# Where the last squares of a norm are added, and which PSUM banks three projection jobs of an indexer use

## The chip, the cores and the metric

The kernel runs on one core of a Trainium2 chip. The metric is the device time of one execution, in microseconds. A core has several engines, each with its own queue of instructions: TensorE (PE, matrix products; its weight loads are listed as PEld), VectorE (DVE), ScalarE (ACT), GpSimd (POOL) and SyncE (SP, which issues DMAs). Matrix products are written to PSUM, which is divided into banks; the other operands lie in SBUF. An engine that needs what another makes waits on a semaphore.

## What is computed

A decoder trunk of two layers, 512 tokens (T) of 1024 features (D), in float32. Each layer has a half-step SwiGLU (inner width 2816), a mixer, and another half-step SwiGLU; layer 0's mixer is a hybrid of an SSD and an mLSTM group, layer 1's is sparse attention with an indexer that picks 128 keys per query. Each of the six parts begins with a norm over the features.

```python
def rms_norm(x, g):
    y = x * lax.rsqrt(jnp.mean(x * x, axis=-1, keepdims=True) + EPS) * g
    return y

for l in range(2):
    x = x + 0.5 * swiglu(rms_norm(x, ffn_norm[l, 0]), ...)
    h = rms_norm(x, mix_norm[l])
    m = hybrid_mixer(h, ...) if l == 0 else sparse_attention(h, cos, sin, sa_w_in, ...)
    x = x + m
    x = x + 0.5 * swiglu(rms_norm(x, ffn_norm[l, 1]), ...)

def sparse_attention(h, ...):
    q, k, v, qi, ki, wi = split_cols(h @ w_in, (1024, 64, 64, 512, 64, 8))
    # rope and norms of q, k, qi, ki
    logits = einsum('bthd,bsd->btsh', qi, ki)
    score = einsum('btsh,bth->bts', relu(logits), wi) * idx_scale
    # causal mask; the top k keys of each query; softmax attention over these
    return o @ w_out
```

## The kernel before

**Layout.** The residual x lies transposed in SBUF: eight chunks (j = 0 to 7) of 128 features x 512 tokens. Products of float32 are made as three matmuls (`mm3`, lines 241 to 243) of a rounded part and a remainder: `form` tiles hold the two parts of a weight, `xgn` those of the normed input. A remainder is a subtraction on VectorE (L363 for weights and others, L660 for xgn), the rounded part a copy on ScalarE (L361, L657).

**Stages.** In program order: ffn00, mix0 (hybrid), ffn01, ffn10, mix1 (attention), ffn11. `Plan` collects the steps of the whole program with an estimated duration each and the keys that they read and write. `order` then walks through time: for each engine it takes, of the steps that are ready, the one that can start first, and among those the one with the earlier due time, which is propagated back from TensorE's steps. TensorE's steps keep their order within a stream (the attention stage has more than one; with them, other rules for due times hold). So a step with another cost or another dependency moves others on every engine.

**A norm that is settled late.** The mean of squares isn't awaited before the next stage's products begin: xgn is x times the gain, without the norm's factor, and the factor is multiplied in behind the products. Two functions do that for five norms (mix0, ffn01, ffn10, mix1, ffn11):

- `prep_later` (from L633) is called for two chunks at a time, as x becomes final. For each chunk it makes xgn's two parts and, on ScalarE, the square (L669). The squares of the earlier chunks are added into `ssq` by GpSimd (L356 with POOL, 128x512 or halves of it). The squares of the last call, two chunks, are kept apart in the list `ssqs`: with `ssq` that makes three operands.
- `settle_later` (L612 to L631) is called at two points of the next stage. At the first, `sums` (L327) has TensorE add over the 128 partitions: for each of four token blocks, one matmul with a column of ones for each operand, 12 for three operands. The result `pssq` is 128x4. VectorE turns it into mean + eps (L624), GpSimd raises it to the power -0.5 (L626). At the second point, TensorE transposes the factor into rows (`prow`, L336) and ScalarE copies them to `rrow` (L630), which VectorE multiplies to the products (L444 and others). In mix1 there are no rows; there ScalarE scales the columns directly (L1595).

The places of these two points are set by code: in `unit`, the first unit of an FFN stage, whose products into `pg` and `pu` go in blocks of 12 matmuls of 128x512, they come behind the blocks at positions 1 and 3, in ffn11 (`late`) behind those at 2 and 4. In the hybrid it is `unit_eight` and its column positions that set them. In mix1 they are the points around `scaled`.

**Layer 1's indexer.** In `attention`, `indexer(jobs, ks)` projects the normed input by the columns for ki, qi and wi (`iw`, widths 64 and 292). There are seven jobs, one for each token block b and half g (block 0 has one of 64 columns). The first four go together into banks of `gm`, `po` and twice `lg`, ahead of the norm's sums in mix1. Behind the sums, the last three follow one by one, each with `scaled`, its evacuation by ScalarE (L1595). Their banks are `gm`, `po`, `gm`: the third needs the bank that the first of the last three leaves. `self.bank(tag)` takes the next bank of a tag's ring; `lg` has three, `pt` two, `gm` and `po` one each. Further on `gm` is the bank of the key-value projection (`gm<-xgn,form`), `lg` that of the indexer's logits (L1665), `pt` that of the scores summed over heads (L1656), `pq` that of transposes (L1521). Then come rope on VectorE (L1507 to L1511), the diagonal weights on GpSimd (L1648), the selection of keys (L1883 and L1884 on VectorE) and the heads.

Of the kernel before, what the change touches and what calls it, by code (L numbers as in the profile page):

```python
# [13 lines left out]
ALU = mybir.AluOpType  # L14
# [4 lines left out]
NB = T // P  # L19
# [194 lines left out]
class Trunk:  # L214
# [135 lines left out]
    def t(self, us, issue, reads, writes):  # L350
        self.plan.add("tensor", us, issue, reads, writes)
# [224 lines left out]
    def unit(self, raws, stream, late, summed):  # L576

        nc, rrow = self.nc, self.rrow  # L580
        ps = self.pair("pg", "pA"), self.pair("pu", "pB")
        f = []
        for qs in ((0, 1), (2, 3)):
            for i in range(4):
                for _ in range(2 if not f else 1):
                    next(stream, None)
                xg, xgk = self.xg, self.xgk
                if len(f) < 4:
                    f.append(self.made(raws[i], i >= summed))
                j, b = f[i]  # L590
                for s in range(2):
                    col = slice(s * P, (s + 1) * P)
                    for q in qs:
                        k = 2 * q + i % 2
                        self.times(
                            *ps[i // 2], s, (j, lambda b=b, q=q, col=col: (b[:, 0, q, col], b[:, 1, q, col])),
                            lambda k=k: (xg[0][k], xg[1][k]), xgk(k), q == 0 and i % 2 == 0, q == 3 and i % 2 == 1, False, T,
                            0.693,
                        )
                if 2 * qs[0] + i in ((2, 4) if late else (1, 3)):  # L600
                    self.settle_later()
        yield
        t, tk = self.place()
        g = lambda: t()[:, 4:8].rearrange("p (s a) b -> p s (a b)", s=2)
        h = lambda: t()[:, 0:4].rearrange("p (s a) b -> p s (a b)", s=2)
        r = lambda: rrow.unsqueeze(1).to_broadcast([P, 2, T])
        gk, hk = ([tk(a + i) for i in range(4)] for a in (4, 0))
        pk = lambda ps: [(*ps[1], 0), (*ps[1], 1)]
        self.vtt(2 * T, g, ps[0][0], r, ALU.mult, gk, pk(ps[0]) + ["rrow"])
        self.s(2 * T, lambda: nc.scalar.activation(g(), g(), AF.Silu), gk, gk, AF.Silu)  # L610
        self.vtt(2 * T, h, ps[1][0], r, ALU.mult, hk, pk(ps[1]) + ["rrow"])
        self.vtt(2 * T, h, h, g, ALU.mult, hk, hk + gk)  # L612
        yield t, tk
# [20 lines left out]
    def prep_later(self, which, k, last, squares=True, half=None):  # L634

        nc = self.nc
        if k == 0 and not half:  # L640
            self.which = which
            self.xgn = [[Lazy(lambda: self.part.tile([P, 4, T], F32R, name="xgn", tag="xg")) for _ in range(2)] for _ in range(2)]
            squares4 = Lazy(lambda: self.tmp.tile([P, 4, T], F32, name="ssq", tag="ssq", bufs=1))
            self.sqs = [lambda i=i: squares4()[:, i] for i in range(4)]
            self.ssq = self.sqs[0]
            self.ssqs, self.ssqk = [(self.ssq, 0)], ["ssq"]
            self.xg = [LazyFeat(t) for t in self.xgn]
            self.xgk = lambda k: [("xg", which, i, k) for i in range(2)]
        xgn, xT, ssq = self.xgn, self.xT, self.ssq
        halves = (0, 1) if half is None else (half,)  # L650
        cols = slice(halves[0] * H, halves[-1] * H + H)
        n = cols.stop - cols.start
        for j in (k, k + 1):
            g, x = self.gain(which, j), xT[:, j, cols]
            hi, lo = (lambda i=i, j=j: xgn[i][j // 4]()[:, j % 4, cols] for i in range(2))
            hik, lok = ([("xg", which, i, j)] for i in range(2))
            self.s(n, lambda hi=hi, x=x, g=g: nc.scalar.activation(hi(), x, AF.Copy, scale=g), self.xk(j, halves), hik)  # L657

            def low(hi=hi, lo=lo, x=x, g=g, j=j):
                nc.vector.scalar_tensor_tensor(lo(), x, g, hi().bitcast(F32), op0=ALU.mult, op1=ALU.subtract)  # L660

            self.v(n, low, self.xk(j, halves) + hik, lok)
            if not squares:
                continue
            if j == 0:
                sq, sk = ssq, ["ssq"]
            else:
                sq, sk = self.sqs[1 + j % 3], [("sq", j % 3)]
            self.s(n, lambda x=x, sq=sq: nc.scalar.activation(sq()[:, cols], x, AF.Square), self.xk(j, halves), sk)  # L669
            if last:  # L670
                self.ssqs, self.ssqk = self.ssqs + [(sq, halves[0] * NB // 2)], self.ssqk + sk
            elif j:
                part = [lambda x=x: x()[:, cols] for x in (ssq, sq)]
                self.vtt(n, part[0], *part, ALU.add, ["ssq"], ["ssq"] + sk, True)
        if last:
            self.pending = 1 + squares

# [859 lines left out]
    def attention(self, nxt):  # L1537
# [9 lines left out]
        iw, last = [], len(plan.steps) - 1  # L1547
        for c0 in (QI0, QI0 + N1):
            for k0, k1 in ((0, 3), (3, 6), (6, 8)):
                if k1 == KC:  # L1550
                    plan.floor = last
                n = k1 - k0
                i, raw = self.ring("raw")
# [38 lines left out]
        def scaled(jobs):  # L1592
            for b, g, (ps, psk) in jobs:
                cols = slice(0 if b else KI - N1, N1 if b else KI - N1 + 64)
                self.s(cols.stop - cols.start, lambda b=b, g=g, ps=ps, cols=cols: act(  # L1595
                    pr[b][0]()[:, g * N1 + cols.start : g * N1 + cols.stop], ps()[:, cols], AF.Copy, scale=rcol[:, b : b + 1]
                ), [psk, "rcol"], [pr[b][1]])
# [5 lines left out]
        self.settle_later()  # L1603
        rcol = self.rcol
        scaled(jobs)
        for b, g, tag in ((2, 1, "gm"), (3, 0, "po"), (3, 1, "gm")):
            jobs = [(b, g, self.bank(tag))]
            indexer(jobs, (0, 1, 2, 3, 6, 7, 4, 5))
            scaled(jobs)
# [17 lines left out]
        for b in range(NB):  # L1627
            t, xk = pr[b]
            c0, n = (0, 9) if b else (KI, 1)
# [12 lines left out]
            n, sc, sk = (b + 1) * P, mask[b], maskk[b]  # L1642
# [320 lines left out]
```

## Time and profile before

| | us |
|---|---|
| timed, median of 3 runs | 2012.17 (2010.16 to 2013.01) |
| the profiled execution | 2003.96 |
| its span in the trace | 2002.2 |
| granted clock of TensorE, mean | 0.992 |
| VectorE / ScalarE / GpSimd busy | 1627.8 / 1264.7 / 325.0 |

In the rows of the profile a time is in microseconds from the span's start; an operation is named by the line of the kernel, the engine and `out<-in`. In a row of the timeline the first number is the start, the second how long the instructions named in it take together (xN), and what is in brackets is the idle time of the engine just before them and who released it. A matmul of the program with float32 operands gives two records, so the 12 sums of a norm are 24 records.

### The profile page before, as it was taken

To read this page: it belongs to the slowest core of one execution; us is meant where nothing else is said; L and a number is where in the kernel's file an instruction comes from. 1 tells how busy PE (TensorE), PEld (TensorE's weight loads), DVE (VectorE), ACT (ScalarE), POOL (GpSimd) and SP (SyncE) were. 2 spreads that over 40 slices of the span, in tenths; PEclk is the share of its full clock that TensorE was granted. 3 is DMA by queue.
4 is the path that set the end of the run, shared out by engine and by line. 5 is a ranking of instruction groups with operands and counts; after the bars stand their busy time and mean duration, and the time that the engine had idled before them with its cause. 6 is when DMAs were issued, how large, how long until landed. Compare 5 with 4: busy or idle time off the path is not lost.

```text
span 2002.2 us, 36425 instructions
## 1 busy us (share of the span) xinstructions
PE 1956.5 (98%) x14674; PEld 1813.3 (91%) x14674; DVE 1627.8 (81%) x2373; ACT 1264.7 (63%) x1906; POOL 325.0 (16%) x401
## 2 busy tenths in 40 slices
PE   8999999999999999999999999999999999999998
PEld 6999999799888888999998999999866588999998
DVE  6888888887888558989788998878589647988886
ACT  6666656567777545766566566666747744757564
POOL 1000002222234110000012001001414521101010
PEclk9999999999999999999999999999899999999999
DMA  8566766467769342666654466565735202666564
GB/s 221 137 157 152 176 155 161 118 166 190 198 176 262 86 117 74 162 172 162 158 149 141 111 170 161 155 174 137 188 88 116 53 17 69 158 158 169 148 170 115
DMA packets 226609, 292.89 MB, mean 146 GB/s; under 512 B 15036, under 2 KB 196488, under 8 KB 225928
## 3 DMA queue, kind: packets, MB, share of 16 engines
q1 hardware_dynamic: 200728, 199.30, 32.2%
q0 software_dynamic: 25632, 91.24, 24.2%
q8 instruction: 115, 1.88, 0.4%
q14 instruction: 54, 0.44, 0.1%
q10 hardware_dynamic: 80, 0.02, 0.0%
HBM read 192.96 MB, written 6.33 MB: 100 GB/s over the span
## 4 chain that ended last, share of the span: by engine, by line
PE 76%; DVE 8%; DMA 8%; issue 5%; ACT 1%; POOL 1%; SPq 0%; POOLq 0%; ACTq 0%; DVEq 0%
PE pA L242 9%; PE pA L241 9%; PE pA L243 9%; PE pD L241 5%; PE pD L243 5%; PE pD L242 5%; DMA form<-raw 3%; PE hm L242 2%; PE hm L243 2%; PE hm L241 2%; PE pB L241 2%; PE pB L243 2%; PE pB L242 2%; DMA raw<-in_hy_w_in 2%; DVE raw L356 2%
## 5 line engine op out<-in xcount | busy, mean ns | idle before, releaser
L363 DVE TENSOR_TENSOR form<-raw,form 128x1024 fp32r<-128x1024 f32 (+2 forms) x382 | 454.9, 1195 | 101.5 <-ACT form L361 100.0
L361 ACT ACTIVATE form<-raw 128x1024 fp32r<-128x1024 f32 (+2 forms) x382 | 392.1, 1030 | 206.0 <-DVE raw L356 142.4
L392 POOL DMA_DIRECT2D form<-raw x172 | 150.9, 879 | 1344.3 <-ACT form L391 1298.3
L356 DVE TENSOR_TENSOR raw<-raw 128x1024 f32<-128x1024 f32 (+2 forms) x281 | 333.2, 1190 | 22.8 <-DMA raw<-in_ffn_w_down 9.0
L241 PE MATMUL pA<-xf,form 128*128 128x256 f32 x1152 | 321.2, 279 | 0.0
L243 PE MATMUL pA<-xf,form 128*128 128x256 f32 x1152 | 320.7, 278 | 0.0
L242 PE MATMUL pA<-xf,form 128*128 128x256 f32 x1152 | 320.7, 278 | 0.0
L391 ACT ACTIVATE form<-raw 128x1024 fp32r<-128x1024 f32 (+1 forms) x172 | 178.2, 1037 | 161.6 <-PE pD L243 74.4
L241 PEld LDWEIGHTS pA<-xf,form 128*128 128x128 f32 x1152 | 217.2, 188 | 0.3
L243 PEld LDWEIGHTS pA<-xf,form 128*128 128x128 f32 x1152 | 217.3, 189 | 0.0
L242 PEld LDWEIGHTS pA<-xf,form 128*128 128x128 f32 x1152 | 217.0, 188 | 0.2
L242 PE MATMUL pA<-hid,form 128*128 128x256 f32 x704 | 198.2, 282 | 3.3 <-DVE hid L363 3.3
L241 PE MATMUL pA<-hid,form 128*128 128x256 f32 x704 | 198.0, 281 | 0.6 <-ACT hid L361 0.5
L243 PE MATMUL pA<-hid,form 128*128 128x256 f32 x704 | 197.2, 280 | 0.0
L393 ACT ACTIVATE form<-raw 128x1024 fp32r<-128x1024 f32 (+1 forms) x172 | 176.5, 1027 | 0.0
L241 PE MATMUL pD<-xf,form 128*128 128x256 f32 x576 | 160.3, 278 | 0.0
L243 PE MATMUL pD<-xf,form 128*128 128x256 f32 x576 | 160.2, 278 | 0.0
L242 PE MATMUL pD<-xf,form 128*128 128x256 f32 x576 | 160.2, 278 | 0.0
L356 DVE TENSOR_TENSOR ft<-ft 128x256 f32<-128x256 f32 (+2 forms) x296 | 151.3, 543 | 3.6
L242 PEld LDWEIGHTS pA<-hid,form 128*128 128x128 f32 x704 | 132.4, 188 | 5.2 <-DVE hid L363 5.1
L241 PEld LDWEIGHTS pA<-hid,form 128*128 128x128 f32 x704 | 132.6, 188 | 1.4 <-ACT hid L361 0.7
L508 ACT ACTIVATE ft<-pA 128x512 f32<-128x512 f32 x120 | 71.5, 595 | 97.7 <-PE pA L243 90.0
(441 smaller groups left out, 5427.6 us busy)
## 6 DMA issues: line engine op xcount, KB each, us to landing
form<-raw POOLq DMA_DIRECT2D x156, 512.0 KB, 5.9
raw<-in_ffn_w_gate SPq DMA_DIRECT2D x88, 512.0 KB, 3.9
raw<-in_ffn_w_up SPq DMA_DIRECT2D x88, 512.0 KB, 4.1
raw<-in_ffn_w_down SPq DMA_DIRECT2D x64, 512.0 KB, 4.0
raw<-in_hy_w_in SPq DMA_DIRECT2D x44, 512.0 KB, 4.7
raw<-in_ffn_w_down SPq DMA_DIRECT2D x32, 384.0 KB, 3.1
raw<-in_hy_w_out SPq DMA_DIRECT2D x16, 512.0 KB, 4.2
form<-raw POOLq DMA_DIRECT2D x16, 384.0 KB, 4.2
```

The lines of the kernel that those rows point to most:

```text
L241: mm(out, l[0], r[0], start=start, stop=False)
L242: mm(out, l[0], r[1], start=False, stop=False)
L243: mm(out, l[1], r[0], start=False, stop=stop)
L356: (self.p if pool else self.v)(n, lambda: e.tensor_tensor(out(), x(), y(), op=op), reads, writes)
L361: self.s(n, lambda: nc.scalar.activation(hi(), src(), AF.Copy), srck, hik)
L363: n, lambda: nc.vector.tensor_tensor(lo(), src(), hi().bitcast(F32), op=ALU.subtract), srck + hik, lok
L391: self.s(n, lambda: nc.scalar.activation(f()[:, 1], raw, AF.Copy, scale=-1.0), rawk, lok)
L392: self.plan.add("gpsimd", 0.85, lambda: nc.gpsimd.dma_start(f()[:, 1], raw, accum_op=ALU.add), rawk + lok, lok, 5.5)
L393: self.s(n, lambda: nc.scalar.activation(f()[:, 0], raw, AF.Copy), rawk, hik)
L508: self.s(T, lambda: nc.scalar.activation(to(), ps()[:, :, 0:H], AF.Copy), [(*psk, 0), (*psk, 1)], tok)
```

## The change

Three places of the code change.

```diff
@@ unit
-                if 2 * qs[0] + i in ((2, 4) if late else (1, 3)):
+                if 2 * qs[0] + i in ((2, 4) if late else (2, 3)):
                     self.settle_later()
@@ prep_later
-            if last:
-                self.ssqs, self.ssqk = self.ssqs + [(sq, halves[0] * NB // 2)], self.ssqk + sk
-            elif j:
+            if j:
                 part = [lambda x=x: x()[:, cols] for x in (ssq, sq)]
-                self.vtt(n, part[0], *part, ALU.add, ["ssq"], ["ssq"] + sk, True)
+                self.vtt(n, part[0], *part, ALU.add, ["ssq"], ["ssq"] + sk, not last)
@@ attention
-        for b, g, tag in ((2, 1, "gm"), (3, 0, "po"), (3, 1, "gm")):
+        for b, g, tag in ((2, 1, "pt"), (3, 0, "pt"), (3, 1, "lg")):
```

The squares of the last two chunks are now added into `ssq` like the others, but by VectorE; `ssqs` keeps one operand, so the sums are 4 matmuls rather than 12, and they read what VectorE added. In `unit` the first point moves one block of 12 matmuls on in ffn01 and ffn10, the second stays. The last three indexer jobs take banks of `pt`, `pt` and `lg`. All lines behind L670 move up by two: L716 of the changed kernel is L718 before, L1023 is L1021, and so on.

The plan orders the steps anew. First VectorE at mix0's norm, the end of the residuals of ffn00 (`raw<-pA`), the remainders of xgn, weight forms, and the mean (L624). Before:

```order
L718 SCALAR_TENSOR_TENSOR raw<-pA,raw 128x2x256
L660 SCALAR_TENSOR_TENSOR xgn<-raw,xgn 128x512 x4
L363 TENSOR_TENSOR form<-raw,form 128x1024
L1023 COPY raw<-hc 128x76
L363 TENSOR_TENSOR form<-raw,form 128x1024 x2
L1032 TENSOR_SCALAR raw<-raw 128x16
L624 TENSOR_SCALAR raw<-pssq 128x4
```

And of the change:

```order
L716 SCALAR_TENSOR_TENSOR raw<-pA,raw 128x2x256
L660 SCALAR_TENSOR_TENSOR xgn<-raw,xgn 128x512 x4
L363 TENSOR_TENSOR form<-raw,form 128x1024 x3
L356 TENSOR_TENSOR ssq<-ssq 128x512 x2
L363 TENSOR_TENSOR form<-raw,form 128x1024
L624 TENSOR_SCALAR raw<-pssq 128x4
L1021 COPY raw<-hc 128x76
```

The two additions stand behind three forms, and the copy of the gates (`hc`) comes behind the mean rather than two forms ahead of it. A form that stood ahead of the last four remainders before is among the three now.

Second, VectorE at ffn11's norm, where the last products of the attention's output projection (`lg`) are added to the residual. Before:

```order
L356 TENSOR_TENSOR raw<-lg,raw 128x256 x2
L660 SCALAR_TENSOR_TENSOR xgn<-raw,xgn 128x512
L356 TENSOR_TENSOR raw<-lg,raw 128x256
L660 SCALAR_TENSOR_TENSOR xgn<-raw,xgn 128x512 x3
L624 TENSOR_SCALAR raw<-pssq 128x4
```

And of the change:

```order
L356 TENSOR_TENSOR raw<-lg,raw 128x256 x2
L660 SCALAR_TENSOR_TENSOR xgn<-raw,xgn 128x512
L356 TENSOR_TENSOR raw<-lg,raw 128x256
L660 SCALAR_TENSOR_TENSOR xgn<-raw,xgn 128x512
L356 TENSOR_TENSOR ssq<-ssq 128x512 x2
L660 SCALAR_TENSOR_TENSOR xgn<-raw,xgn 128x512 x2
L624 TENSOR_SCALAR raw<-pssq 128x4
```

The additions stand behind one remainder that follows the last residual. On TensorE the sums follow directly on the last `lg` products in both; 24 matmuls into `pu` stand between sums and transposes before, and 12 of these stand ahead of the last 39 `lg` products now.

Third, TensorE at mix1's norm, from the last product of the four joint jobs (`lg`) through the sums to the next job. Before:

```order
L242 MATMUL lg<-iw,xgn 128x292
L243 MATMUL lg<-iw,xgn 128x292
L327 MATMUL pssq<-raw,ssq 128x1 x12
L241 MATMUL gm<-iw,xgn 128x292
L242 MATMUL gm<-iw,xgn 128x292
```

And of the change:

```order
L242 MATMUL lg<-iw,xgn 128x292
L243 MATMUL lg<-iw,xgn 128x292
L327 MATMUL pssq<-raw,ssq 128x1 x4
L241 MATMUL pt<-iw,xgn 128x292
L242 MATMUL pt<-iw,xgn 128x292
```

Behind this, 12 matmuls of the job stand ahead of the first transpose of ki (`pq<-raw,ri`) before, and 45 now. The first 12 matmuls of the key-value projection (`gm<-xgn,form`), which stood behind the logits of token block 1 (128x256), stand among them now; on VectorE the rope of block 3, which stood behind the first pair of the key selection, stands ahead of it; and on GpSimd the 16 diagonal weights of blocks 1 and 2 are made in one go, ahead of the DMAs of the query weights (before, 14 of them).

## The prediction

> **What bounds the kernel now.** I read the page from the top, then TensorE's waits, then the five places where a norm is settled.
>
> ```profile
> span 2002.2 us, 36425 instructions
> PE 1956.5 (98%) x14674; PEld 1813.3 (91%) x14674; DVE 1627.8 (81%) x2373; ACT 1264.7 (63%) x1906; POOL 325.0 (16%) x401
> PE 76%; DVE 8%; DMA 8%; issue 5%; ACT 1%; POOL 1%; SPq 0%; POOLq 0%; ACTq 0%; DVEq 0%
> ```
>
> TensorE (PE) is busy 1956.5 of 2002.2 us, and 76% of the chain that ends last is its own work. It can win time in three ways only: fewer instructions, fewer waits, or a higher granted clock. The next rows are those of its waits that the change comes near: what TensorE was about to run, for whom it waited, us in all, how often, and the longest.
>
> ```profile
> PE pq L1521 <- DVE q L1511: 3.7, 2, 3.0
> PE gm L242 <- DVE iw L363: 3.4, 1, 3.4
> PE pg L242 <- DVE xgn L660: 2.7, 3, 1.0
> PE hc L242 <- DVE xgn L660: 2.1, 2, 1.3
> PE pssq L327 <- POOL ssq L356: 0.9, 1, 0.9
> PE pq L1521 <- ACT ri L1533: 0.8, 1, 0.8
> ```
>
> Waits at the sums themselves (L327) come to 0.9 us. So what the sums cost is their own time on TensorE, and what they do to the clock. The first is seen at the hybrid mixer's norm (mix0):
>
> ```profile
> L327 PE MATMUL pssq<-raw,ssq x120: 164/250/352, 359.1 to 1664.4; 128*128 128x1 f32 x120
> 359.12 2.73 PE L327 MATMUL pssq<-raw,ssq 128*128 128x1 f32 x24
> 361.71 0.48 PE L241 MATMUL hm<-xgn,form 128*128 128x512 f32 x1
> ...
> 362.83 0.63 PE L242 MATMUL hm<-xgn,form 128*128 128x512 f32 x1
> ...
> 366.14 0.60 PE L336 MATMUL prow<-raw 128*128 128x128 f32 x4
> ```
>
> Each of the five norms has 24 records of one column. Here they hold TensorE 2.7 us, from 359.12 to about 361.8, or 0.112 us each. Then come 12 wide matmuls, from 361.71 to 366.14. They take 4.4 us, and from 362.83 on each lasts 0.63 us where others have 0.39 to 0.48. The windows show that this is the granted clock (columns: us, busy us of the five engines, granted clock, DMA share, GB/s):
>
> ```profile
> 1085.00:1093.00 8.00, 8.00 (x49) 7.06 (x48) 4.87 (x7) 1.14 (x2) 1.47 (x1) 1.00 0.62 197
> 362.00:366.20 4.20, 4.20 (x13) 3.19 (x12) 0.04 (x1) 0.00 (x0) 1.04 (x1) 0.59 0.30 88
> 1434.00:1445.00 11.00, 10.21 (x56) 9.35 (x55) 5.35 (x12) 6.70 (x15) 8.14 (x14) 0.69 0.68 212
> 1663.00:1672.70 9.70, 9.70 (x34) 7.99 (x35) 0.69 (x2) 0.00 (x0) 1.02 (x1) 0.65 0.01 2
> 1535.00:1570.00 35.00, 29.32 (x153) 14.66 (x151) 29.16 (x101) 31.28 (x81) 22.71 (x37) 1.00 0.27 54
> 1565.00:1580.00 15.00, 12.01 (x66) 7.52 (x63) 8.89 (x23) 9.78 (x25) 9.23 (x13) 0.89 0.00 0
> ```
>
> Behind three norms (362, 1434, 1663) the clock falls to 0.59, 0.69 and 0.65; behind ffn10's (1085) it stays at 1.00. The loss is 4.2 x 0.41 = 1.7 us, 11 x 0.31 = 3.4 us and 9.7 x 0.35 = 3.4 us. I read these as half clock, since a stretch of one-column matmuls gives the array little work. At full clock the 12 wide matmuls would take 4.4 - 1.7 = 2.7 us: the price of one block below. (The last two windows are for later.)
>
> [...] The row at 359.12 has no idle time ahead of it and the clock fell all the same, so the trace favours a window that counts work done; whether it falls then depends on the window's phase.
>
> **The change, part by part.**
>
> *Fewer sums, all five norms.* 12 matmuls of the program become 4, so 24 records become 8. 16 x 0.112 = 1.8 us is saved at each norm, 9.0 us in all, all of it on TensorE. What it costs is two additions of 128x512 on VectorE, and that the sums now wait for them. The rows of ffn01 give the sums as they stand, the nearest price of one addition, the form and the square beside it, and the power on GpSimd for all norms:
>
> ```profile
> 750.17 2.73 PE L327 MATMUL pssq<-raw,ssq 128*128 128x1 f32 x24
> 748.31 0.69 DVE L356 TENSOR_TENSOR raw<-hm,raw 128x512 f32<-128x512 f32 x1 [2.38 <-PE hm L243]
> 749.18 1.23 DVE L363 TENSOR_TENSOR form<-raw,form 128x1024 fp32r<-128x1024 f32 x1 [0.17 <-ACT form L361]
> 749.05 0.62 ACT L669 ACTIVATE ssq<-raw 128x512 f32<-128x512 f32 x1
> L626 POOL TENSOR_TENSOR raw<-raw x5: 1017/1032/1471, 362.1 to 1665.0; 128x4 f32<-128x4 f32 x5
> ```
>
> One addition is 0.7 us, a pair 1.4. VectorE, busy 81%, has ten more instructions, 7 us.
>
> *ffn01.* The last square ends at 749.7, the form at 750.4; behind it the addition ends near 751.1, and even with a microsecond lost by 752.1. By the new order one block of 12 wide matmuls, 2.7 us, is issued ahead of the sums, so TensorE reaches them near 750.17 + 2.7 = 752.9 and doesn't wait. Behind the sums only one block is left to cover the mean (0.2 us) and the power on GpSimd (L626, 1.0 to 1.5 us): 2.7 us against at most 1.7 and the handing over. I take **1.6 us**, 0.2 being lost where pg waits for a later L660 (bounds 1.1, if a whole addition of 0.7 is lost so, and 1.8).
>
> *ffn10.* The additions stand ahead of the last two L660 before the mean. TensorE's sums, the last L660s and the last squares of before are
>
> ```profile
> 1085.14 2.74 PE L327 MATMUL pssq<-raw,ssq 128*128 128x1 f32 x24
> 1085.92 2.06 DVE L660 SCALAR_TENSOR_TENSOR xgn<-raw,xgn 128x512 fp32r<-128x512 f32 x3
> 1083.76 1.16 ACT L669 ACTIVATE ssq<-raw 128x512 f32<-128x512 f32 x2 [1.74 <-DVE raw L718]
> ```
>
> The squares are there at 1084.9. One L660 and the pair end at 1085.92 + 0.7 + 1.4 = 1088.0. TensorE came to the sums at 1085.1 and comes one block later now, 1087.8. The wait is 0.2, and the mean, behind two more L660 on VectorE, is ready near 1089.5; the power takes up to 1.5 more, 1091.0, while TensorE reaches the transposes (L336) at 1088.0 + 0.9 + 2.7 = 1091.6. 1.8 - 0.2 gives **1.6 us** (0.1 if the mean is a form and a power of 1.5 us later, 1.8 if all is hidden).
>
> *mix0.* Here the sums keep their place, and VectorE has three forms (L363) ahead of the additions, one more than stands below behind the last L660s.
>
> ```profile
> 352.41 3.10 DVE L660 SCALAR_TENSOR_TENSOR xgn<-raw,xgn 128x512 fp32r<-128x512 f32 x3
> 356.72 2.34 DVE L363 TENSOR_TENSOR form<-raw,form 128x1024 fp32r<-128x1024 f32 x2
> 357.04 0.62 ACT L669 ACTIVATE ssq<-raw 128x512 f32<-128x512 f32 x1
> ```
>
> If the forms end as now, at 359.06, the additions end at 360.45, and the sums that stood at 359.12 wait 1.35 us. One form that stood ahead of the last L660s stands behind them now, and so the wait of hc for xgn (2.1 us in all) can shrink by up to its 1.2 us (2.34 for two). Without the fall of the clock the transposes come at 360.5 + 0.9 + 2.7 = 364.1, or 2.0 us earlier, and 3.2 with the earlier start; with the fall, 1.7 less: 0.3 to 1.5. I take no fall, since the work lost to sums shrinks from 2.7 to 0.9 us, and the middle: **2.5 us** (0.3 to 3.2).
>
> *mix1.* TensorE doesn't wait for the additions: VectorE idles 8 us there.
>
> ```profile
> 1432.66 0.16 DVE L624 TENSOR_SCALAR raw<-pssq 128x4 f32<-128x4 f32 x1 [8.03 <-PE pssq L327]
> 1429.89 2.73 PE L327 MATMUL pssq<-raw,ssq 128*128 128x1 f32 x24
> 1435.72 0.48 PE L1521 MATMUL pq<-raw,ri 128*128 128x128 f32 x1 [0.79 <-ACT ri L1533]
> ```
>
> 1.8 us of sums go. The three projection jobs with banks of their own run on behind the sums, 45 matmuls in a row ahead of the first pq (before, 12), so the 0.8 us wait is gone too. With a full window behind the sums the 3.4 us of half clock go: 6.0 us by the time of the indexer's logits. Late next are the heads, 1535 to 1570, where TensorE has 29.3 of 35 us busy and VectorE 29.2, ScalarE 31.3. The order also moves 12 wide matmuls (2.7 us) of the key-value product ahead, out of the stretch in which they covered VectorE. So I take 1.5 us as given back: **4.5 us** (1.1, where clock stays low and part is given back, to 6.0).
>
> *ffn11.* TensorE has 12 wide matmuls ahead of the last block of the out projection, where before it had them behind the sums, and then nothing between that block and the sums.
>
> ```profile
> 1661.16 3.55 PE L327 MATMUL pssq<-raw,ssq 128*128 128x1 f32 x24 [0.88 <-POOL ssq L356]
> 1672.62 0.60 PE L336 MATMUL prow<-raw 128*128 128x128 f32 x4
> 1660.32 0.42 DVE L356 TENSOR_TENSOR raw<-lg,raw 128x256 f32<-128x256 f32 x1 [0.35 <-PE lg L243]
> 1660.84 0.63 ACT L669 ACTIVATE ssq<-raw 128x512 f32<-128x512 f32 x1 [0.19 <-DVE raw L356]
> ```
>
> From the end of the block (1661.16 - 0.88 = 1660.28) to the transposes are 12.3 us. In the new order: 2.7 for the moved block, then a wait for residual (0.4), square (0.6) and the pair (1.4) with some 0.3 us of handing over, 2.7 in all, then 0.9 of sums and 2.7 of the other block: 9.0 us, 3.3 less. But 2.7 us of idleness and 0.9 of sums are as long a lull as 0.9 and 2.7 were, and cost half clock again: 3.4 us if as long as now (0.1 us slower), 1.7 if for half of it (1.6 faster). Between these two, **0.7 us** (-0.1 to 3.3).
>
> *The rest.* On VectorE the residuals (L718) and forms around 1410 change places, ahead of the 3.4 us wait of gm for iw; as many stand ahead of each iw form as before, within one. I take 0 (bounds 0.7 either way, one L718). GpSimd loses nothing but order; its diagonals move ahead of the weights' DMAs.
>
> The sum is 1.6 + 1.6 + 2.5 + 4.5 + 0.7 = **10.9 us**. The profiled execution took 2003.96 us, span 2002.2 and 1.8 around it, and lies 8.2 us under the median of the timed ones; I take the gain off both: 1993.1 profiled, 2012.2 - 10.9 = **2001.3 us** timed.
>
> **Rivals.**
>
> *The clock doesn't follow the sums.* For it: behind two norms of five the clock did not fall although the sums were the same, and the phase of the windows shifts with everything ahead. Then mix0 and mix1 keep their loss, 1.7 and 3.4 us, the latter partly given back already: 10.9 - 1.7 - 2.6 = 6.6 us, 2005.6. [...]
>
> *All falls vanish.* ffn11 gets 3.3, mix1 its 6.0 and mix0 3.2: with 1.6 twice 15.7 us, 1996.5. For it: the lulls shrink everywhere but in ffn11; against it: ffn11's.
>
> *It comes to nothing.* The sums are shorter but wait for VectorE at every norm: 1.35 in mix0, and as much in ffn01 and ffn10 when L660 or a form stands longer ahead of the additions; the heads give back the rest, for they are bound by VectorE and ScalarE. That is 9.0 - 3 x 1.35 - 2.7 = 2.2 us, 2010.0. Against it: ACT's squares and the idle 8 us of VectorE in mix1.
>
> *Slower.* The heads at 1535 to 1570 wait for VectorE's ropes (L1511) and what the key-value product covered is used up sooner. Idle time there is 5.7 us now, with one wait of 3.0. Each wait over about 3 us also brings 1.7 us of half clock (1565 to 1580: 15 x 0.11, with the wait of 3.0 in it). The gain of 10.9 is undone if 11 us are added there, which takes three waits of 2 us more, each with a fall; 2.7 us of moved matmuls don't pay for that. Four such waits would be 4 x 3.7 = 14.8 us, 2016.1.
>
> **How the numbers follow.** I give the forecast 0.45, the rival with the clock unmoved 0.22, all falls gone 0.14, nothing 0.13, slower 0.06. The range goes from 1993.5, the third case with the bounds of the rest, to 2009.5, near the fourth: it leaves out some 0.2. A measurement of this kernel can tell about 0.2%, 4 us, from no change: the first three cases lie beyond it, so faster 0.81, within 0.13, slower 0.06.
>
> **What would show it.** L327 x40 rather than x120, and ten additions of 0.7 us on ssq. Of the clock: 1.00 in the windows behind mix0's and mix1's sums, and a fall behind ffn11's. Of the waits: TensorE for ssq on VectorE 1 to 1.4 us in mix0 and near 2.7 in ffn11, none for L626; the pq wait on ri gone. If the sums wait in ffn01 or ffn10, or idle time at 1535 to 1570 grows by over 3 us, my terms there are wrong; if the clock falls behind mix1's sums as before, its cause is.

## The result, and the profile after

| | before | changed |
|---|---|---|
| timed, median, first measure of both (6 runs each) | 2011.16 us | 1991.32 us |
| ratio of that measure, 95% interval | | 0.9893 (0.987 to 0.9916) |
| ratio of a second and a third measure | | 0.9935 (0.9914 to 0.9956), 0.9921 (0.9895 to 0.9947) |
| all executions of the experiments: mean, median | 2007.8, 2007.6 us (87 of them) | 1992.8, 1992.6 us (23) |
| mean granted clock of these executions | 0.9913 | 0.9936 |
| profiled execution, its span | 2003.96, 2002.2 us | 1992.64, 1990.8 us |

The kernel became faster, by 15.0 us between the means (0.75%, standard error 1.0), where 10.9 was forecast. The time lies just below the range (1993.5 to 2009.5). The two profiled executions differ by 11.3 us; single executions scatter by more than that, from 1996.8 to 2020.2 us before and from 1986.4 to 2003.1 changed.

The page of the changed kernel, the lines that answer to those of before:

```profile
span 1990.8 us, 36264 instructions
PE 1944.0 (98%) x14594; PEld 1800.1 (90%) x14594; DVE 1631.5 (82%) x2383; ACT 1268.3 (64%) x1906; POOL 320.2 (16%) x401
PE 78%; DVE 8%; DMA 7%; issue 4%; ACT 1%; POOL 1%; ACTq 0%; DVEq 0%; POOLq 0%; SPq 0%
```

TensorE has 80 records fewer, VectorE ten instructions more, and TensorE's own work still sets the end. TensorE's waits that answer to those shown of before are these (what it was about to run, for whom it waited, us, times, longest):

```profile
PE pssq L327 <- DVE ssq L356: 4.0, 2, 2.9
PE pA L243 <- DVE form L363: 3.4, 1, 3.4
PE pg L242 <- DVE xgn L660: 2.5, 3, 1.0
PE hc L242 <- DVE xgn L660: 1.8, 2, 1.0
PE gm L242 <- DVE oh L1832: 1.5, 1, 1.5
```

The wait for `iw` near 1414 has only changed its name (pA for a form, 3.4 us again). New is the wait of the sums for VectorE's additions, 4.0 us in two places (before, they waited 0.9 us for GpSimd). Gone are the waits of pq for q (3.7 us) and for ri (0.8). The sums and additions themselves, by line and tile:

```profile
L327 PE MATMUL pssq<-raw,ssq x40: 164/250/250, 360.5 to 1657.1; 128*128 128x1 f32 x40
L356 DVE TENSOR_TENSOR ssq<-ssq x10: 678/688/694, 359.0 to 1655.5; 128x512 f32<-128x512 f32 x10
```

40 records in place of 120, ten additions of 0.69 us. And the windows behind the norms, with the granted clock in the third column from the end:

```profile
360.40:364.40 4.00, 3.89 (x22) 3.35 (x23) 1.48 (x4) 0.00 (x0) 1.05 (x1) 1.00 0.22 64
1430.00:1445.00 15.00, 15.00 (x110) 13.98 (x109) 5.39 (x13) 9.26 (x20) 10.57 (x18) 1.00 0.73 198
1535.00:1570.00 35.00, 31.94 (x179) 17.33 (x180) 31.33 (x102) 32.71 (x85) 23.50 (x33) 1.00 0.16 31
1565.00:1580.00 15.00, 15.00 (x93) 9.31 (x94) 9.67 (x28) 12.17 (x23) 8.58 (x12) 1.00 0.55 131
1656.00:1661.00 5.00, 4.66 (x18) 3.87 (x19) 1.59 (x4) 0.00 (x0) 1.03 (x1) 0.66 0.00 0
```

Behind mix0's and mix1's sums the clock stays at 1.00 now (before: 0.59 and 0.69 in such windows). Behind ffn11's it still falls. In the heads, 1535 to 1570, TensorE is busy 31.9 us of 35 rather than 29.3, and the fall behind 1570 is gone.

### The profile page after: what moved, and what is told of

Read it like the earlier page. It is cut to its first block, busy times and chain, and to the rows that moved or that the text cites. A ratio compares the mean times of both kernels' runs of the same rounds, so it can differ in the third digit from the quotient of the medians.

```text
span 1990.8 us, 36264 instructions
## 1 busy us (share of the span) xinstructions
PE 1944.0 (98%) x14594; PEld 1800.1 (90%) x14594; DVE 1631.5 (82%) x2383; ACT 1268.3 (64%) x1906; POOL 320.2 (16%) x401
## 4 chain that ended last, share of the span: by engine, by line
PE 78%; DVE 8%; DMA 7%; issue 4%; ACT 1%; POOL 1%; ACTq 0%; DVEq 0%; POOLq 0%; SPq 0%
PE pA L242 9%; PE pA L243 9%; PE pA L241 9%; PE pD L243 5%; PE pD L241 5%; PE pD L242 5%; DMA form<-raw 3%; PE hm L241 3%; PE hm L242 3%; PE hm L243 3%; PE pB L241 2%; PE pB L243 2%; PE pB L242 2%; DVE form L363 2%; PE pg L242 1%
## 5 line engine op out<-in xcount | busy, mean ns | idle before, releaser
L242 PEld LDWEIGHTS pA<-hid,form 128*128 128x128 f32 x704 | 132.7, 188 | 6.1 <-DVE hid L363 6.0
L243 PEld LDWEIGHTS pA<-hid,form 128*128 128x128 f32 x704 | 132.9, 189 | 3.6 <-DVE form L363 3.6
L241 PEld LDWEIGHTS pA<-hid,form 128*128 128x128 f32 x704 | 133.0, 189 | 2.2 <-ACT hid L361 1.1
```

Of the source, the lines that this page charges most:

```text
L241: mm(out, l[0], r[0], start=start, stop=False)
L242: mm(out, l[0], r[1], start=False, stop=False)
L243: mm(out, l[1], r[0], start=False, stop=stop)
```

## The experiments

Twelve runs; the table gives them all but the clock kernel, which is no version of the trunk. "Full clock" is the time multiplied by the granted clock of the same execution, and so roughly what is left without the clock's losses; for before it is 1990.2, for the changed kernel 1980.0 us. The ratio is to executions of before that ran beside the kernel, in the same job.

| run | executions | mean us | clock | full clock us | ratio, 95% interval |
|---|---|---|---|---|---|
| before again (e0) | 12 | 2008.6 | 0.9908 | 1990.2 | 1.0009 (0.9988 to 1.0031) |
| banks only (e1) | 12 | 1999.9 | 0.9925 | 1984.9 | 0.9966 (0.995 to 0.9982) |
| squares only (e2) | 7 | 1995.7 | 0.9934 | 1982.5 | 0.9941 (0.992 to 0.9962) |
| squares and settling points (e3) | 8 | 1996.1 | 0.9936 | 1983.4 | 0.9948 (0.9929 to 0.9966) |
| changed, again (f1) | 9 | 1995.1 | 0.9930 | 1981.2 | 0.9935 (0.9914 to 0.9956) |
| changed, a third time (g0) | 8 | 1991.6 | 0.9941 | 1979.9 | 0.9921 (0.9895 to 0.9947) |
| changed, sums three times (f4) | 12 | 2006.4 | 0.9912 | 1988.7 | 0.9988 (0.9967 to 1.0008) |
| before, other order, 1.40 (f5) | 12 | 2000.8 | 0.9928 | 1986.4 | 0.9963 (0.9944 to 0.9983) |
| before, other order, 1.30 (g2) | 12 | 1999.6 | 0.9921 | 1983.8 | 0.9962 (0.9943 to 0.9981) |
| changed, other order, 1.40 (g4) | 10 | 1995.4 | 0.9937 | 1982.8 | 0.9937 (0.9913 to 0.9961) |
| changed, block put back (g1) | 6 | 1988.5 | 0.9947 | 1977.8 | 0.9905 (0.9872 to 0.9937) |

### Before, again

No edit.

> The kernel before, run again as a kernel of its own, so that its executions come with their granted clock. The two profiled executions differ by 11.3 us, the timed medians by about 20. Theory A (the profiled execution of before happened to lose less clock than its timed ones): mean clock of these executions near 0.988, against 0.991 to 0.997 for the changed kernel's, and time falling by about 1.5 to 2 us for each 0.001 of clock; a second profile shows its half-clock stretches at other places than the first. Theory B (the spread comes from waits for DMA): clock about as high as the changed kernel's, 0.992 to 0.996, and no tie between clock and time.

Its twelve executions go from 1997.01 us at a clock of 0.994 to 2019.55 at 0.988; a line through them falls 2.5 us for each 0.001 of clock, one through the 26 of before in that job 1.8. So the clock carries most of the scatter: theory A holds in that, and the forecast's profile, at 0.992, was one of the better executions. The mean clock, 0.9908, lies between what the two theories asked for. And the second profile has its half clock at the places of the first, behind the sums of mix0, mix1 and ffn11 (in the first at 362.6, 1434.4 and 1663.1 us), in the hybrid (615.2), ahead of mix1's sums (1417.3) and in the heads (1570.9), with ffn10's sums as the one new place; other places had been expected. But the first three timings (median 2012.17) were above the 2007.6 of all, and the pooled clock differs from the changed kernel's by 0.0023 only, some 4.7 us. The clock alone doesn't make 15.

### One part of the change alone

Banks only (e1):

```diff
-        for b, g, tag in ((2, 1, "gm"), (3, 0, "po"), (3, 1, "gm")):
+        for b, g, tag in ((2, 1, "pt"), (3, 0, "pt"), (3, 1, "lg")):
```

> Before with only the three PSUM banks changed: sums, squares and the settling points as before. By the prediction's terms the banks save the 0.8 us wait of pq and at most part of mix1's half clock: 1 to 3 us faster than before (ratio 0.9985 to 0.9995). Rival (the attention's new order is where the gain comes from): 8 us or more faster (ratio 0.996 or lower), with the gain in the heads after 1530 us.

0.9966, or 7 to 8 us: between the two numbers and far nearer to the rival's. On TensorE its order is that of before up to mix1's sums, so the gain lies behind them: from these sums to the end its profile takes 565.2 us, that of before 572.3.

Squares only (e2):

```diff
-            if last:
-                self.ssqs, self.ssqk = self.ssqs + [(sq, halves[0] * NB // 2)], self.ssqk + sk
-            elif j:
+            if j:
...
-                self.vtt(n, part[0], *part, ALU.add, ["ssq"], ["ssq"] + sk, True)
+                self.vtt(n, part[0], *part, ALU.add, ["ssq"], ["ssq"] + sk, not last)
```

> The last squares added by VectorE, 4 sums in place of 12 per norm; the settling points and the banks as before. By the prediction's terms: 9.0 us of sums, less waits for the additions of 1.4 us in mix0, about 2 in ffn01 and 2.9 in ffn10 (which now have no block ahead of the sums), and some clock: 5 to 9 us faster (ratio 0.9955 to 0.9975), with L327 waiting for VectorE's ssq in ffn01 and ffn10. Rival (clock is the gain): 12 us or more faster, mean clock 0.994 or more.

0.9941, 12 us: more than the forecast's terms give, at the rival's lower end, and the clock (0.9934) is just under what the rival asked. The sums wait for VectorE 5.3 us in three places, 2.6 of it in ffn11, 1.1 in mix0 and 1.7 in ffn10; I had put about 6 on ffn01, ffn10 and mix0 alone, so those waits were overrated.

Squares and settling points (e3): as e2, with `(2, 3)` for `(1, 3)` in `unit`.

> Squares and settling points changed, banks as before. By the prediction's terms about 10.9 less the banks' 1 to 3 us: 8 to 10 us faster than before (ratio 0.995 to 0.996), the waits of L327 in ffn01 and ffn10 gone. Rival (the banks' order is the gain): within 4 us of before.

0.9948, or 10 to 12 us: just above the forecast, and the rival is out. Against e2 the moved point is worth nothing that these runs can tell. Neither this nor the banks is the whole gain; the parts add to more than the whole (7.9 by the means for the banks, 11.7 for this, together 19.6 where the changed kernel has 15.0), so they share something. What they share is in the section on the order below: each of them moves the instructions of the heads.

### The price of the sums

The changed kernel with every norm's sums issued three times over:

```diff
-            self.t(0.2 + 0.45 * len(ssqs), lambda: self.sums(ps(), [(x(), b) for x, b in ssqs]), self.ssqk, ["pssq"])
+            self.t(0.2 + 0.45 * len(ssqs), lambda: [self.sums(ps(), [(x(), b) for x, b in ssqs]) for _ in range(3)], self.ssqk, ["pssq"])
```

> The changed kernel, with each norm's four sums issued three times over, into the same columns with the same operand: 24 records per norm again, and the order of every other instruction as in the changed kernel. By the prediction's term: 16 x 0.112 = 1.8 us per norm, 9.0 us in all, and the clock falls more often behind the sums (mean clock lower by 0.001 to 0.003, 2 to 5 us): 9 to 14 us slower than the changed kernel, so 4 to 10 us faster than before. Rival (the sums cost little, the order is the gain): within 5 us of the changed kernel.

11.3 us slower than the changed kernel of the same job, 13.6 than all of its executions. At full clock the difference is 7.5 or 8.7 us, where 9.0 had been worked out from 0.112 us a record; the other 3.8 or 4.9 are clock. That part came as expected; the other did not: against before the kernel is not 4 to 10 but 2.4 us faster (1.4 by all executions). It keeps the changed order of the heads, but the waits of the sums for VectorE too (4.0 us in its profile). The mean clock is that of before again (0.9912 and 0.9913), so the clock that the change wins hangs on the sums. In this execution it falls behind the sums of mix0, ffn01 and ffn11, but not behind mix1's:

```profile
361.00:372.00 11.00, 9.92 (x51) 8.20 (x50) 4.25 (x8) 0.60 (x2) 1.05 (x1) 0.84 0.41 128
1430.00:1450.00 20.00, 20.00 (x159) 20.00 (x158) 10.54 (x21) 13.37 (x23) 11.91 (x16) 1.00 1.01 251
1663.00:1676.00 13.00, 10.41 (x39) 9.34 (x40) 3.83 (x7) 1.90 (x4) 1.53 (x2) 0.61 0.07 25
```

These are windows of this kernel around the sums of mix0, mix1 and ffn11: 0.84, 1.00 and 0.61.

Each run left one profile, and together they tell how often the clock falls. The measure is the granted clock of the 15 us from the start of the sums, for the four norms other than ffn11, where idle time ahead of the sums comes in. With 24 records (two profiles of before, banks only, the two other orders of before below, sums three times) it is below 1.00 behind 14 of 24 sums: 5 of 6 in mix0, 4 of 6 in mix1, 3 in ffn01, 2 in ffn10. With 8 records (the seven other profiles) it is so behind 2 of 28, both in the kernel with squares only, where the sums had waited 1.1 and 1.7 us for VectorE. The mean loss behind 24 records is 1.1 us for each norm. Three of these windows at mix0, of the two other orders of before (1.40 and 1.30) and of the changed kernel:

```profile
359.00:374.00 15.00, 15.00 (x73) 12.61 (x73) 7.07 (x13) 4.34 (x8) 1.03 (x1) 0.89 0.29 82
360.00:375.00 15.00, 15.00 (x79) 12.73 (x79) 8.71 (x14) 5.81 (x10) 1.04 (x1) 1.00 0.28 76
361.00:376.00 15.00, 15.00 (x70) 12.31 (x70) 10.78 (x19) 6.37 (x10) 1.59 (x2) 1.00 0.43 141
```

### What lowers the clock

A kernel of its own:

```python
for name, (before, steps, behind) in PARTS.items():
    for c in range(40):
        n = 14 + (c * 5) % 9          # wide matmuls, 128x512
        for i in range(n): matmul(acc, wide, back)
        sums(before)                  # 12, 8 or 4 matmuls of one column
        if steps: ...                 # TensorE waits for 4 or 2 steps of ScalarE
```

> No part of the trunk: TensorE runs 14 to 22 wide matmuls (128x512, 3.2 to 5 us) in turn with a lull, 40 times for each of six lulls: 24, 16 and 8 records of one column (2.7, 1.8 and 0.9 us), an idle time of about 2.6 us, one of about 1.4 us, and one of 2.6 us with 8 records of one column behind it. The output is zeros. Theory A (the clock's window counts work, and one-column matmuls count for little): half clock behind part of the 24-record lulls, at least as often as behind idle time of the same length; rarely or never behind 8 records or 1.4 us. Rival (only idle time counts): none behind the one-column lulls, however long.

One execution. The windows of the first five parts, in their order (24, 16 and 8 records; idle gaps of 2.7 and of 1.4 us as they came out):

```profile
20.00:280.00 260.00, 260.00 (x1453) 227.48 (x1453) 0.00 (x0) 0.00 (x0) 0.00 (x0) 0.90 0.00 1
290.00:515.00 225.00, 225.00 (x1295) 196.23 (x1295) 0.00 (x0) 0.00 (x0) 0.00 (x0) 1.00 0.00 1
525.00:740.00 215.00, 215.00 (x1124) 182.88 (x1123) 0.00 (x0) 0.00 (x0) 0.00 (x0) 1.00 0.00 1
750.00:1070.00 320.00, 211.86 (x714) 158.02 (x713) 0.00 (x0) 98.11 (x158) 0.00 (x0) 0.87 0.00 0
1080.00:1290.00 210.00, 159.05 (x655) 120.23 (x656) 0.00 (x0) 44.36 (x73) 0.00 (x0) 1.00 0.00 0
```

In the first part TensorE is never idle (260.00 of 260.00 us busy), and the clock is 0.90: a half-clock stretch begins behind 14 of its 39 lulls. With 16 or 8 records it stays at 1.00. An idle gap of 2.7 us costs more, 0.87, with half clock behind 22 of 40; one of 1.4 us costs nothing. So the rival is out, and theory A holds in that matmuls of one column count for little: 0.90 without any idle time. The window that it names is to be seen in before's profile; the last section has the numbers. Not as expected is that 24 records lower the clock less often than idle time of the same length. A lull of 24 records costs 260 x 0.10 / 39 = 0.7 us on average, one of 2.7 us idle time about 320 x 0.13 / 40 = 1.0. The scheduler put the matmuls of the sixth part elsewhere than meant, and it is left out.

### Another order of the same instructions

Before, with another estimate of one step in the plan, which moves instructions in the stretch from the indexer to the heads and changes nothing else:

```diff
-            self.t(n * 1.36e-3 + 0.01, lambda: self.mm3(...
+            self.t(n * 1.40e-3 + 0.01, lambda: self.mm3(...
```

> Before, with only the plan's estimate for a product of the attention stage changed (1.40 in place of 1.36 ns per column): the same instructions, in another order from the indexer to the heads. Theory C (the waits in the heads, such as the 3.0 us of pq for q and the clock behind it, are an accident of before's order that most other orders don't have, and the banks' gain is of this kind): 3 to 7 us faster than before, with that wait gone. Rival (the banks gain by what they do: no wait for an evacuation): within 2 us of before.

0.9963. And a second draw, 1.30 in place of 1.40:

> Before with the plan's estimate for a product of the attention stage at 1.30 in place of 1.36 ns per column: a second other order of the same instructions. Theory C (before's order of the heads is a bad draw; most others lack its 3.0 us wait): 3 to 8 us faster than before. Rival (orders scatter both ways, and 1.40 was a good draw): between 3 us slower and 3 us faster.

0.9962. Both are 7 to 8 us faster than before, as much as the banks alone. The waits of TensorE from mix1's sums to the heads' end show the larger part of it. Before has there, besides the two of pq shown with the prediction,

```profile
PE lg L1784 <- ACT rq L1527: 1.1, 1, 1.1
PE po L1824 <- DVE raw L1788: 0.8, 1, 0.8
PE gm L241 <- DVE raw L624: 0.3, 1, 0.3
PE pt L1521 <- POOL pw L1806: 0.2, 1, 0.2
```

which makes 6.9 us; the second draw has in the same stretch only

```profile
PE lg L1784 <- DVE raw L1788: 1.1, 1, 1.1
PE pq L1521 <- ACT ri L1533: 0.7, 1, 0.7
PE gm L242 <- DVE oh L1834: 0.3, 1, 0.3
PE gm L241 <- DVE raw L624: 0.3, 1, 0.3
```

2.4 us, without the long wait for q. The same window of the heads, of before and of this draw, differs accordingly: 1565 to 1580 had 12.01 us of TensorE busy and a clock of 0.89, and now

```profile
1565.00:1580.00 15.00, 15.00 (x93) 8.87 (x89) 9.80 (x24) 12.90 (x27) 10.08 (x15) 1.00 0.24 61
```

The 4.5 us of waits and some 1.7 us of clock (15 x 0.11) make 6.2 of the 7 to 8; the rest isn't placed. Theory C holds: before's order of the heads is a bad draw, and each of four other orders (banks, squares, two estimates) lost the 3.0 us wait. The longest of pq for q that is left in any of them is 1.4; these are the rows of the first draw and of the banks alone:

```profile
PE pq L1521 <- DVE q L1511: 1.4, 1, 1.4
PE pq L1521 <- DVE q L1511: 0.7, 1, 0.7
```

The changed kernel with the estimate of 1.40:

> The changed kernel with the same estimate at 1.40: another order of its instructions from the indexer to the heads. Theory C (its heads have no long wait to lose): within 3 us of the changed kernel, on either side. Rival (the estimate itself makes better orders): 4 us or more faster.

1995.4 us, 2.6 above the mean of all executions of the changed kernel and 3.8 above those of its own job, with the intervals overlapping: no further gain is in this draw.

The changed kernel itself, a third time, beside these:

> The changed kernel a third time, as the measure for the other kernels of this job and for a mean over all its executions. Expected from the fifteen so far: mean 1990 to 1997 us, 12 to 17 us under before. If the first six were lucky, it comes near the second measure (13 us); if not, near 16.

1991.6 us on average, nearer to the first measure than to the second. The second (f1) had been expected at 1989 to 1993 us, or at 1996 or more if the first six executions were lucky; with 1995.1 it came between, nearer to the rival. All 23 executions together make the 15.0 us.

### A block put back behind the out projection

In ffn11 the first block into `pu` gets a late due time, so that it stands behind the last `lg` products:

```diff
+                self.plan.later = 5e3 if self.stage == "ffn11" and self.pending == 2 and i == 2 else 0.0
                 for s in range(2):
...
+                self.plan.later = 0.0
```

> The changed kernel, with one block of 12 wide matmuls into pu put back behind the last block of the attention's output projection in ffn11, so that it stands between that and the sums. The 2.9 us wait of L327 for VectorE's additions in ffn11 shrinks to 0.2 or less, and the lull before and with the sums from 3.8 us to 1: by the clock kernel (half clock behind 34 of 53 idle times of 2.9 us, 1.7 us lost each) about 1 us of clock with it. Theory A: 2.5 to 4.5 us faster than the changed kernel. Rival (what the wait saves is given back where the mean is awaited, at the transposes or at VectorE): within 1 us of it.

TensorE in the changed kernel, from the last product of the out projection to the transposes:

```profile
1653.16 0.28 PE L243 MATMUL lg<-oh,wq 128*128 128x256 f32 x1
1656.34 1.02 PE L327 MATMUL pssq<-raw,ssq 128*128 128x1 f32 x8 [2.90 <-DVE ssq L356]
...
1658.04 0.63 PE L243 MATMUL pu<-xgn,form 128*128 128x512 f32 x1
...
1661.65 0.60 PE L336 MATMUL prow<-raw 128*128 128x128 f32 x4
```

And with the block put back:

```profile
1656.32 0.28 PE L243 MATMUL lg<-oh,wq 128*128 128x256 f32 x1
1656.43 0.40 PE L241 MATMUL pu<-xgn,form 128*128 128x512 f32 x1
...
1659.53 1.02 PE L327 MATMUL pssq<-raw,ssq 128*128 128x1 f32 x8
...
1663.06 0.40 PE L243 MATMUL pu<-xgn,form 128*128 128x512 f32 x1
1663.29 0.60 PE L336 MATMUL prow<-raw 128*128 128x128 f32 x4
```

The wait of 2.90 us is covered, and the matmuls behind the sums last 0.40 rather than 0.63 us (granted clock 1.00 from 1656 to 1664; in the changed kernel 0.66 from 1656 to 1661). From the last `lg` to the transposes are 6.97 us with 24 wide matmuls in between, where the changed kernel needs 8.49 with 12: 1.5 us less for 2.75 us more work, so 4.3 won. The stretch ahead of it, from mix1's sums to that `lg`, gets shorter by the moved work (219.0 us, 221.7 before the block was put back), so nothing is lost there. By the totals it is 4.3 us under the changed kernel (3.1 under that of its own job), at the upper end of what was expected, with a standard error of 2.2 and overlapping intervals: the trace shows the gain, the totals are no proof of it. Its mean is the lowest here.

## Why the prediction was right at the norms and wrong at the heads and in its base

Point by point, from the traces; where 12 wide matmuls were moved into or out of a stretch, their 2.75 us are reckoned in.

| place | forecast | measured |
|---|---|---|
| mix0, first hc to transposes | 2.5 us | 19.34 to 16.21: 3.1 |
| ffn01, sums to transposes | 1.6 | 8.19 to 3.66 + 2.75: 1.8 |
| ffn10, the same | 1.6 | 8.16 to 4.01 + 2.75: 1.4 |
| mix1, sums to last product of the out projection | 4.5 | 230.1 to 221.7 - 2.75: 11.1 |
| ffn11, that product to transposes | 0.7 | 12.62 to 8.49 + 2.75: 1.4 |

*The norms* came as worked out in their own places. In mix0 the sums waited 1.1 us (forecast 1.35) and the clock stayed up (1.00 from 360.4 to 364.4); in ffn01 and ffn10 they didn't wait, though in ffn10 the transposes waited 0.5 us for the power (L626), where no wait was forecast; in ffn11 the sums waited 2.9 us (forecast 2.7), and the lull cost clock again (half clock for 3.41 us, from 1657.4 on). The sums' own time was right (7.5 to 8.7 us against 9.0).

```profile
360.51 1.02 PE L327 MATMUL pssq<-raw,ssq 128*128 128x1 f32 x8 [1.10 <-DVE ssq L356]
754.80 0.94 PE L327 MATMUL pssq<-raw,ssq 128*128 128x1 f32 x8
1089.45 1.02 PE L327 MATMUL pssq<-raw,ssq 128*128 128x1 f32 x8
```

*The step that failed* is mix1's term, 4.5 us where 11.1 were measured, in the words "Late next are the heads" and "So I take 1.5 us as given back". The heads gave nothing back; they won. In the changed kernel TensorE waits from the sums to the heads' end for

```profile
PE gm L242 <- DVE oh L1832: 1.5, 1, 1.5
PE lg L1782 <- ACT pT L1525: 0.6, 1, 0.6
PE pt L1519 <- POOL pn L1804: 0.5, 1, 0.5
```

2.6 us, 4.3 less than before's 6.9. With 1.8 us of sums and 5.1 us of clock (3.4 behind the sums, 1.7 behind the long wait of the heads) that makes the 11.1 but for 0.1. Of these the prediction had 6.0, less 1.5. I took the heads' waits for a bound that VectorE's work sets (29 of 35 us busy), while they were a matter of one order: the row of the 3.0 us wait was quoted, its clock too, and I used both only for the slower rival, as something that more of could come. The experiments with another order settle that: the same instructions, 7 to 8 us less. The profiles agree on this stretch from one execution to the next, while the stretch ahead of it scatters:

| profile | first of mix1's sums at, us | from there to the span's end, us |
|---|---|---|
| before, two executions | 1429.9, 1437.1 | 572.3, 572.3 |
| changed, three executions | 1431.4, 1435.9, 1432.3 | 559.4, 558.6, 559.7 |
| banks only | 1435.0 | 565.2 |
| before, other orders (1.40, 1.30) | 1440.5, 1431.7 | 564.3, 566.2 |
| squares only; squares and settling points | 1437.0; 1426.3 | 563.5; 563.6 |
| changed, sums three times | 1438.8 | 566.2 |
| changed, other order | 1431.0 | 562.2 |
| changed, block put back | 1437.3 | 554.3 |

From mix1's sums on the change wins 13 us, where 4.5 + 0.7 = 5.2 were forecast. How much of the banks' gain is their own effect can't be told from these runs, since every edit there reorders the heads; against the other draws it isn't to be seen. By the same measure the block put back is worth 4 to 5 us, as its rows say, and the other order of the changed kernel costs some 3.

*The clock's term* was right in its sum, for a reason that needs care. I took from one trace that mix0 and mix1 lose 1.7 and 3.4 us and would win them back, 5.9 us with ffn11's part. By all executions the clock gives 4.7 (17.5 us lost before, 12.8 after). But whether a norm's lull hits differs from one execution to the next: 14 of 24 in the profiles, 14 of 39 in the clock kernel. The right estimate would have been the mean, 1.1 us for each of four norms, ffn01 and ffn10 among them, and not what one execution showed: mix0 loses 1.4 us on average, mix1 1.7, half of its 3.4. That 5.9 and 4.7 come near to each other is luck, in mix1 above all.

*The base* is the second step that failed. The sum was set against a median of three runs that stood 4.5 us above the 87 later ones. From 2007.6, the forecast would have been 1996.7, and the range would have reached down to 1989.0. The two faults add up: too small a gain, taken off too high a time, and both make the forecast too slow. Between the means, 4.4 us of the 8.5 that separate 2001.3 from 1992.8 are the base and 4.1 the gain. The range's lower end isn't what its working says either: the third case with the bounds of the rest gains 15.7 + 0.2 + 0.2 + 0.7 = 16.8 us, which gives 1995.4 and not 1993.5.

*Luck* is that the profiled execution came at 1992.64 us where 1993.1 had been forecast for it: the five places won 18.8 us in it, and 7.5 were lost elsewhere.

*The sum outside the clock.* At full clock the executions differ by 10.2 us (1990.2 to 1980.0). The sums save 9.0, they wait 3.1 us more (4.0 against 0.9), and TensorE waits 4.3 us less from mix1's sums to the heads' end: 10.2 again. The waits are those of one profile each and other waits moved too, so that it agrees so well is chance.

*What stays open.* The five places sum to 18.8 us, the executions to 15.0, the two profiles to 11.3. In the profiles the rest was lost elsewhere: half clock between mix0 and ffn01 (3.41 us at 527.6 and 6.83 at 616.4, where before has 3.41 at 615.2) and ahead of mix1's sums (6.83 us at 1415.1, before 3.41 at 1417.3), and waits of hm for DMA (7.8 us against 5.0). The profiles of the other runs say the same of all executions: of the 15.0 us some 13 lie behind mix1's sums, and so only some 2 ahead of them, where mix0, ffn01 and ffn10 won 6.3 in their places and 5.7 were forecast. Such differences also stand between runs of the same order: TensorE's instructions agree up to mix0's sums in all versions, and the first hc began at

```profile
346.80 0.39 PE L241 MATMUL hc<-xgn,form 128*24 128x512 f32 x1
352.05 0.40 PE L241 MATMUL hc<-xgn,form 128*24 128x512 f32 x1
```

in before and in a second profile of the changed kernel. Whether the 3 to 4 us that are missing ahead of mix1 are such scatter or a real loss, these runs don't tell.

A correction to the description of before, ahead of the prediction: the positions 2 and 4 (`late`) in `unit` belong to the very first unit of ffn00. In ffn11 the settling points stood at 1 and 3 like those of ffn01 and ffn10, and the change moved the first of them there too. The prediction's working for ffn11 goes by the order of instructions and isn't touched by that.

## What to carry to other kernels

A long wait in a scheduler's output is first to be suspected as one draw of the order: perturb an estimate that changes no work and see whether it stays, before it is read as a bound or as the gain of an edit. A run of one-column matmuls cost its own time here (0.112 us a record) and, with 24 records, in part of the cases the clock of the work behind it (half clock behind 14 of 39 in the clock kernel; with 16, behind none of 40). So shorten such a run, or put wide matmuls where TensorE would wait ahead of it, as the block put back does (clock 1.00 rather than 0.66 behind the sums), and see in the trace whether the clock stays. Take the base of a forecast from many executions, and clock losses as a mean over several traces rather than from one. When executions scatter, look for a stretch whose length repeats from profile to profile, and compare that.

## What the runs showed of the hardware that was not expected

TensorE busy without a gap was no guard of its clock: in the clock kernel 24 one-column records in a row (2.7 us) brought half clock behind 14 of 39 lulls (0.90 on average in that part), 16 in a row (1.8 us) behind none of 40 (1.00). An idle gap of 2.7 us lowered it behind 22 of 40 (0.87), one of 1.4 us never (1.00). In the profiles of before and of the changed kernel the half clock comes in stretches of 3.41 us (seven) or 6.83 us (four), but for one that the end of each cuts short: in before the granted clock is 0.50 throughout from 362.6 to 366.0 and from 1434.4 to 1441.2, and 3.4 us of it cost 1.7.

The window and its phase, of which the prediction and theory A speak, show in the same profile of before. Between 1400 and 1700 us its half clock begins at 1417.30, 1434.38, 1570.90 and 1663.06, so 17.08, 136.52 and 92.16 us apart: 5, 40 and 27 times some 3.41. In steps of that length, laid so that they end where half clock begins, one step holds nearly all of mix0's sums (2.68 us of them, 359.17 to 362.58), while those of ffn01 and of ffn10, as long, fall into two steps each (748.29 to 755.11 and 1082.79 to 1089.62). Besides the sums TensorE is busy for 0.73 us in mix0's step, 1.49 in the one ahead of mix1's fall (1430.96 to 1434.37) and 0.64 in ffn11's (1659.65 to 1663.06); in the four of ffn01 and ffn10, behind which the clock stays at 1.00, it is 1.74 to 2.2 us. TensorE was busy all through mix0's step (3.41 of 3.41 us), so no idle time lowered the clock there. Behind TensorE's waits of 3.4 us for iw and of 3.0 us for q, half clock follows for 3.41 us (from 1417.30 and from 1570.90). A window that counts work, and one-column matmuls for little, fits all five norms of this profile.

The power on four columns (L626), 1.0 us in four norms of the changed kernel, took 2.6 us in ffn10's in one profile, and the transposes then waited 0.5 us for it. The two other profiles of the same kernel don't repeat it (1.5 at most); that of the kernel with the block put back does (2.6). Why it takes longer these runs don't show:

```profile
L626 POOL TENSOR_TENSOR raw<-raw x5: 1032/1033/2622, 361.8 to 1657.7; 128x4 f32<-128x4 f32 x5
```
